# Storing the last slab of a rotary embedding whole instead of in two halves

## Chip, cores and metric

One core of one Trainium2 chip. The metric is the device time of one launch in microseconds (us), the median of several runs. The span in a profile is shorter by about 1.8 us (162.2 against 160.4 in the profiled run of the kernel before). Runs are marked fast or slow by state.

In the profile, a transfer's *issue* is the instruction that starts it, a *packet* is one piece of it (here one descriptor is one packet), and its *landing* is the moment when its completion is fully counted on its *semaphore*, a counter on which instructions can wait (in the traces each transfer makes 16 counts).

## The reference

`x` is (16, 512, 1024) float32, taken as 16 heads of 64; `cos` and `sin` are (512, 32).

```python
x1, x2 = x[..., :half_dim], x[..., half_dim:]
rotated = np.concatenate([
    x1 * cos - x2 * sin,
    x1 * sin + x2 * cos
], axis=-1)
```

33.55 MB come in and 33.55 MB go out, with a few operations for each element.

## The kernel before

The tensor is worked in 8 slabs of 4 MB: 128 partitions with 8192 float32 (32 KB) each. The kernel keeps five slabs on the chip (in SBUF). SyncE loads, ScalarE casts to bfloat16, VectorE does two multiplies and an add, ScalarE casts back and issues the store. The first slab and the last two are computed in halves of 4096 columns. The cuts are marked, here and in the diffs below; some comments are added.

```python
    def dram(t, s, a=0, n=W):          # a..a+n of each partition's 32 KB of slab s
        return bass.AP(tensor=t.tensor, offset=t.offset + s * nb * seq * dim + a,
                       ap=[[W, P], [1, n]])
    ...
    def load(s):
        slab[s] = slabs.tile([P, W], f32, tag="slab", name="slab")
        return nc.sync.dma_start(out=slab[s], in_=dram(x, s))
    ...
    passes = []
    for s in range(nslabs):
        n = rpp if 1 <= s < nslabs - 2 else rpp // 2
        passes += [(s, r, n) for r in range(0, rpp, n)]

    cast(passes[0])
    for i, (s, r, n) in enumerate(passes):
        if i + 1 < len(passes):
            cast(passes[i + 1])        # ScalarE, float32 to bfloat16
        ...                            # VectorE: two multiplies and an add
        back = nc.scalar.copy(out=xs, in_=xu)
        if s == nslabs - 1:
            if r > 0:
                ...                    # keep this copy behind the first half's issue
            part = nc.scalar.dma_start(
                out=dram(out_flat, s, r * dim, n * dim), in_=xs)
        elif r + n == rpp:
            nc.scalar.dma_start(out=dram(out_flat, s), in_=slab[s])
            if s + slots < nslabs:
                load(s + slots)
```

Of the kernel before, what the change touches and what calls it, by code (L numbers as in the profile page):

```python
# [2 lines left out]

# [4 lines left out]


@with_exitstack  # L10
def kernel(
    ctx: ExitStack,
    tc: tile.TileContext,
    x: bass.AP,
    cos: bass.AP,
    sin: bass.AP,
    num_heads: int,
    out: bass.AP,
):
    nc = tc.nc  # L20
    P = nc.NUM_PARTITIONS

    batch, seq, dim = x.shape
    nh = num_heads
    hd = dim // nh
    half = hd // 2
    bf16 = mybir.dt.bfloat16
    f32 = mybir.dt.float32

    nb = 2  # L30
    slots = 5
    nslabs = batch // nb
    rpp = nb * seq // P
    W = rpp * dim
    SP = seq // rpp
    TW = rpp * half

    out_flat = out.rearrange("b s h d -> b s (h d)")

    singles = ctx.enter_context(tc.tile_pool(name="singles", bufs=1))  # L40
    slabs = ctx.enter_context(tc.tile_pool(name="slabs", bufs=slots))
    xpool = ctx.enter_context(tc.tile_pool(name="xpool", bufs=2))
    psum = ctx.enter_context(tc.tile_pool(
        name="psum", bufs=1, space=bass.MemoryType.PSUM))


    def dram(t, s, a=0, n=W):
        return bass.AP(tensor=t.tensor, offset=t.offset + s * nb * seq * dim + a,
                       ap=[[W, P], [1, n]])


    def view(t, offset, *dims):
        return dataclasses.replace(t, offset=t.offset + offset,
                                   ap=[t.ap[0], *[list(d) for d in dims]])


    slab = {}
# [7 lines that stand above are left out]
    load(0)  # L65


    TR = seq // P
    G = rpp // TR
    table = {}  # L70
    raw = singles.tile([P, 2 * TR * half], f32, tag="raw")
    for i, src in enumerate((cos, sin)):
        table[i] = nc.gpsimd.dma_start(out=view(raw, i * TR * half, (1, TR * half)), in_=bass.AP(  # L73
            tensor=src.tensor, offset=src.offset,
            ap=[[TR * half, P], [1, TR * half]]))



    for s in range(1, slots):
        tc.add_manual_dep(  # L80
            load(s).ins, table[0].ins.name,
            mybir.DependencyInfo(mybir.DependencyClass.Sync,
                                 mybir.DependencyReason.DATA),
            reason="issue")



    pick = singles.tile([P, 2 * G * P], bf16, tag="pick")
    nc.gpsimd.memset(pick, 0.0)  # L89
    for g in range(2 * G):  # L90
        part = view(pick, g * P, (SP, P // SP), (1, SP))
        nc.gpsimd.affine_select(  # L92
            out=part, in_=part, compare_op=mybir.AluOpType.not_equal,
            fill=1.0 if g < G else -1.0, base=-(g % G),
            pattern=[[0, P // SP], [-G, SP]], channel_multiplier=1)

    tab1 = singles.tile([P, 2 * TR * half], bf16, tag="tab1")
    nc.gpsimd.tensor_copy(out=tab1, in_=raw)  # L98

    acc = psum.tile([P, 2 * rpp * hd], f32, tag="acc")  # L100
    for i in range(2):
        for h in range(2):
            for g in range(G):
                nc.tensor.matmul(  # L104
                    view(acc, (i * rpp + g * TR) * hd + h * half, (hd, TR), (1, half)),
                    view(pick, (i * h * G + g) * P, (1, P)),
                    view(tab1, i * TR * half, (half, TR), (1, half)),
                    start=True, stop=True)
    tab = singles.tile([P, 2 * rpp * hd], bf16, tag="tab")
    nc.vector.tensor_copy(out=tab, in_=acc)  # L110

    xb = {}


    def cast(u):
        s, r, n = u
        if r == 0:
            xb[s] = xpool.tile([P, W], bf16, tag="xb", name="xb")
        nc.scalar.copy(out=view(xb[s], r * dim, (1, n * dim)),  # L119
                       in_=view(slab[s], r * dim, (1, n * dim)))  # L120
# [13 lines that stand above are left out]
            cast(passes[i + 1])  # L134
        xs = view(slab[s], r * dim, (1, n * dim))
        xu = view(xb[s], r * dim, (1, n * dim))

        t2 = view(slab[s].bitcast(bf16), 2 * r * dim, (1, n * dim))
        for t, a in ((t2, rpp * hd), (xu, 0)):
            nc.vector.tensor_mul(  # L140
                out=t, in0=xu,
                in1=view(tab, a + r * hd, (hd, n), (0, nh), (1, hd)))
        nc.vector.tensor_add(  # L143
            out=xu, in0=xu, in1=view(t2, half, (hd, n * nh), (-half, 2), (1, half)))

        back = nc.scalar.copy(out=xs, in_=xu)  # L146
        if s == nslabs - 1:

            if r > 0:
                tc.add_manual_dep(  # L150
                    back.ins, part.ins.name,
                    mybir.DependencyInfo(mybir.DependencyClass.NoSync,
                                         mybir.DependencyReason.DATA),
                    reason="issue")
            part = nc.scalar.dma_start(
                out=dram(out_flat, s, r * dim, n * dim), in_=xs)
        elif r + n == rpp:
            nc.scalar.dma_start(out=dram(out_flat, s), in_=slab[s])
            if s + slots < nslabs:
                load(s + slots)  # L160


# [1 line left out]
_INS = ['x', 'cos', 'sin', 'num_heads']  # L164
_OUTS = [((16, 512, 16, 64), 'float32')]

_NUMBERS = {'num_heads': 16}


# [26 lines left out]
```

## Time and profile before

| | before |
|---|---|
| median of the 3 runs known at first | 162.57 us (162.40 to 162.63) |
| span of the profiled run | 160.4 us |
| VectorE, ScalarE busy | 68%, 71% |
| loads (q1), stores (q10), share of 16 DMA engines | 49.4%, 48.5% |

The two DMA queues together fill 98% of the span: this kernel moves bytes all the time, and neither compute engine is full. The lines themselves are in the prediction.

### The profile page before, as it was taken

The page shows a single profiled execution, that of the slowest core. Times are in us where ns is not written, and L with a number is a line of the kernel's source. Part 1 is how long each engine was busy: PE and PEld are TensorE (multiplying, and loading weights), DVE is VectorE, ACT ScalarE, POOL GpSimd, SP SyncE. Part 2 cuts the span into 40 slices and gives each one's busy share as a digit, 9 for nine tenths or more (in the row PEclk, how much of TensorE's full clock was granted, in tenths as well). Part 3 has the DMA queues.
Part 4 walks back from the last instruction along what each step waited for, and adds up shares of the span by engine and source line. Part 5 has one row for each costly group of instructions (what it writes and reads, how often), then busy time and mean ns, then how long its engine had stood idle before and what let it go on. Part 6 is the DMA issues. An engine that isn't in the chain of part 4 may idle for free.

```text
span 160.4 us, 169 instructions
## 1 busy us (share of the span) xinstructions
PE 1.0 (1%) x8; PEld 0.8 (1%) x8; DVE 108.5 (68%) x34; ACT 113.5 (71%) x23; POOL 3.4 (2%) x12
## 2 busy tenths in 40 slices
PE   0011000000000000000000000000000000000000
PEld 0010000000000000000000000000000000000000
DVE  0003799999989979997996099939649599920000
ACT  3006939998998999899907997099995999471000
POOL 7000000000000000000000000000000000000000
DMA  7999999999999999999999999999999999999994
GB/s 229 441 409 400 474 433 392 449 466 392 392 392 449 466 392 425 490 392 409 490 409 409 482 417 392 490 425 392 458 458 392 433 482 392 417 490 400 400 437 208
DMA packets 2512, 67.24 MB, mean 419 GB/s; under 512 B 304, under 2 KB 304, under 8 KB 336
## 3 DMA queue, kind: packets, MB, share of 16 engines
q1 hardware_dynamic: 1152, 33.55, 49.4%
q10 hardware_dynamic: 1296, 33.56, 48.5%
q0 software_dynamic: 64, 0.13, 0.2%
HBM read 33.69 MB, written 33.55 MB: 419 GB/s over the span
## 4 chain that ended last, share of the span: by engine, by line
DMA 59%; ACT 17%; issue 9%; DVE 4%; SPq 0%; POOLq 0%
DMA slab<-in_x_dram 40%; DMA out_dram<-slab 15%; ACT slab L146 11%; ACT xb L119 6%; DMA raw<-in_cos_dram 4%; DVE xb L143 1%; DVE xb L140 1%; DVE slab L140 1%; SPq L62 0%; POOLq L177 0%
## 5 line engine op out<-in xcount | busy, mean ns | idle before, releaser
L119 ACT CAST xb<-slab 128x4096 bf16<-128x4096 f32 (+1 forms) x11 | 56.6, 5155 | 27.4 <-DMA slab<-in_x_dram 26.1
L146 ACT CAST slab<-xb 128x4096 f32<-128x4096 bf16 (+1 forms) x11 | 56.6, 5153 | 3.4 <-DVE xb L143 3.4
L140 DVE TENSOR_TENSOR slab<-xb,tab 128x4096 bf16<-128x4096 bf16 (+1 forms) x11 | 35.9, 3260 | 19.7 <-ACT xb L119 19.6
L143 DVE TENSOR_TENSOR xb<-xb,slab 128x4096 bf16<-128x4096 bf16 (+1 forms) x11 | 35.9, 3261 | 0.3
L140 DVE TENSOR_TENSOR xb<-xb,tab 128x4096 bf16<-128x4096 bf16 (+1 forms) x11 | 35.9, 3260 | 0.3
L110 DVE CAST tab<-acc 128x1024 bf16<-128x1024 f32 x1 | 1.2, 1225 | 12.6 <-PE acc L104 12.6
L119 ACT ACT_TABLE_LOAD x1 | 1.3, 1283 | 0.7 <-PEq L177 0.7
L104 PE MATMUL acc<-tab,pick 128*128 128x128 bf16 x8 | 1.0, 305 | 11.6 <-POOL tab L98 11.6
L92 POOL TENSOR_SCALAR_AFFINE_SELECT pick<-pick 128x128 bf16<-128x128 bf16 x4 | 1.0, 289 | 0.1
L104 PEld LDWEIGHTS <-pick 128*128 128x128 bf16 x8 | 0.8, 136 | 11.4 <-issue 8.1
L73 POOL DMA_DIRECT2D raw<-in_cos_dram x1 | 0.7, 677 | 0.8 <-POOLq L177 0.8
L98 POOL CAST tab<-raw 128x256 bf16<-128x256 f32 x1 | 0.4, 398 | 7.0 <-DMA raw<-in_sin_dram 7.0
L89 POOL MEMSET pick<- 128x512 bf16 x1 | 0.5, 544 | 0.0
L73 POOL DMA_DIRECT2D raw<-in_sin_dram x1 | 0.5, 537 | 0.0
L177 POOL MEMSET const-float32-0.0<- 128x1 f32 x1 | 0.1, 99 | 0.2 <-issue 0.2
L177 POOL MEMSET const-bfloat16-1.0<- 128x1 bf16 x1 | 0.1, 102 | 0.0
L177 POOL MEMSET const-uint8-127<- 128x1 uint8 x1 | 0.1, 102 | 0.0
L177 POOL MEMSET const-float32-1.0<- 128x1 f32 x1 | 0.1, 99 | 0.0
## 6 DMA issues: line engine op xcount, KB each, us to landing
slab<-in_x_dram SPq DMA_DIRECT2D x8, 4096.0 KB, 24.6
out_dram<-slab ACTq DMA_DIRECT2D x7, 4096.0 KB, 27.8
out_dram<-slab ACTq DMA_DIRECT2D x2, 2048.0 KB, 15.3
raw<-in_cos_dram POOLq DMA_DIRECT2D x1, 64.0 KB, 7.1
raw<-in_sin_dram POOLq DMA_DIRECT2D x1, 64.0 KB, 9.1
```

The costliest lines, as they stand in the source:

```text
L73: table[i] = nc.gpsimd.dma_start(out=view(raw, i * TR * half, (1, TR * half)), in_=bass.AP(tensor=src.tensor, offset=src.offset, ap=[[TR * ...
L89: nc.gpsimd.memset(pick, 0.0)
L92: nc.gpsimd.affine_select(out=part, in_=part, compare_op=mybir.AluOpType.not_equal, fill=1.0 if g < G else -1.0, base=-(g % G), pattern=[[ ...
L98: nc.gpsimd.tensor_copy(out=tab1, in_=raw)
L104: nc.tensor.matmul(view(acc, (i * rpp + g * TR) * hd + h * half, (hd, TR), (1, half)), view(pick, (i * h * G + g) * P, (1, P)), view(tab1, ...
L110: nc.vector.tensor_copy(out=tab, in_=acc)
L119: nc.scalar.copy(out=view(xb[s], r * dim, (1, n * dim)), in_=view(slab[s], r * dim, (1, n * dim)))
L140: nc.vector.tensor_mul(out=t, in0=xu, in1=view(tab, a + r * hd, (hd, n), (0, nh), (1, hd)))
L143: nc.vector.tensor_add(out=xu, in0=xu, in1=view(t2, half, (hd, n * nh), (-half, 2), (1, half)))
L146: back = nc.scalar.copy(out=xs, in_=xu)
L177: nc = _bacc.Bacc("TRN2", target_bir_lowering=False, num_devices=1)
```

## The change

The intent is to move the last slab in the largest descriptors the layout allows, one of 32 KB for each partition, as for all other slabs, and to give up the early start of its first half in exchange.

```diff
-        back = nc.scalar.copy(out=xs, in_=xu)
-        if s == nslabs - 1:
-
-            if r > 0:
-                tc.add_manual_dep(
-                    back.ins, part.ins.name,
-                    mybir.DependencyInfo(mybir.DependencyClass.NoSync,
-                                         mybir.DependencyReason.DATA),
-                    reason="issue")
-            part = nc.scalar.dma_start(
-                out=dram(out_flat, s, r * dim, n * dim), in_=xs)
-        elif r + n == rpp:
+        nc.scalar.copy(out=xs, in_=xu)
+        if r + n == rpp:
             nc.scalar.dma_start(out=dram(out_flat, s), in_=slab[s])
```

## The prediction

> **What bounds the kernel now.** I read the page first, for who is busy, and in it the shares of the span, the slices and the DMA queues.
>
> ```profile
> span 160.4 us, 169 instructions
> ...
> DVE  0003799999989979997996099939649599920000
> ACT  3006939998998999899907997099995999471000
> ...
> DMA  7999999999999999999999999999999999999994
> ...
> DMA packets 2512, 67.24 MB, mean 419 GB/s; under 512 B 304, under 2 KB 304, under 8 KB 336
> ...
> q10 hardware_dynamic: 1296, 33.56, 48.5%
> ```
>
> The reader is to see that the DMA row holds 9 in every slice but the first and the last, while VectorE and ScalarE have fallen to 0 in the last three slices (about 12 us). The end is not set by the last computation but by transfers still under way. The queue q10 carries the stores; 1296 packets is 7 slabs x (128 descriptors + 16 end markers) = 1008, plus 2 halves x (128 + 16) = 288. So one descriptor is one packet, 32 KB in a whole slab and 16 KB in a half.
>
> Second, the timeline of the end, to see when the last stores are issued.
>
> ```profile
> 131.01 0.34 ACTq L158 DMA_DIRECT2D out_dram<-slab  x1
> ...
> 134.49 3.61 ACT L146 CAST slab<-xb 128x4096 f32<-128x4096 bf16 x1
> ...
> 138.12 0.34 ACTq L155 DMA_DIRECT2D out_dram<-slab  x1
> 139.17 2.29 DVE L143 TENSOR_TENSOR xb<-xb,slab 128x4096 bf16<-128x4096 bf16 x1
> 141.50 3.60 ACT L146 CAST slab<-xb 128x4096 f32<-128x4096 bf16 x1 [3.40 <-DVE xb L143]
> 145.13 0.34 ACTq L155 DMA_DIRECT2D out_dram<-slab  x1
> ```
>
> Slab 6 (the seventh of eight) is issued at 131.01, the first half of slab 7 at 138.12 and the second at 145.13. Third, the view of the output tensor for each of these three moments alone gives issue to landing; in this order:
>
> ```profile
> DMA to landing us min/median/max: 18.6/18.6/18.6
> ...
> DMA to landing us min/median/max: 16.4/16.4/16.4
> ...
> DMA to landing us min/median/max: 14.2/14.2/14.2
> ```
>
> So slab 6 lands at 131.01 + 18.6 = 149.6, the first half at 138.12 + 16.4 = 154.5 and the second at 145.13 + 14.2 = 159.3. The issues lie 7.0 us apart, but the landings 4.9 and 4.8 us: 2.1 MB in 4.85 us is 432 GB/s. The stores stand in line. When the second half is issued, slab 6 is still being written for 149.6 - 145.1 = 4.5 us, and the first half has not moved a byte. The chain of waits ends with the copy at 141.50 and ascribes nothing to that line of transfers, so it is not the view to trust here.
>
> Fourth, the stretches 130 to 148 and 149 to 158.4 (32 KB packets in the first, 16 KB in the second), with busy time of the engines, granted clock, DMA share and GB/s:
>
> ```profile
> 130.00:148.00 18.00, 0.00 (x0) 0.00 (x0) 11.29 (x5) 11.70 (x4) 0.00 (x0) 1.00 1.01 435
> 149.00:158.40 9.40, 0.00 (x0) 0.00 (x0) 0.00 (x0) 0.00 (x0) 0.00 (x0) 1.00 1.00 431
> ```
>
> All 16 engines are full in both. A share a hair over 1 is neighbouring packets that overlap a little and edges of the stretch.
>
> [...]
>
> **The change part by part.**
>
> Removed: the issue at 138.12, 0.34 us on ScalarE's sequencer. ScalarE has nothing to do then: its next copy waits 3.40 us for VectorE's add, which ends at 141.47. Worth 0. Removed too: the ordering of the second copy behind the first issue. The copy runs at 141.50 because of the add, so this is worth 0.
>
> Moved: the first half's bytes are offered at 145.13 instead of 138.12, 7.0 us later. This is the suspected cost. It is paid only if the engines run out of work before. When do they? In the DMA view of the stretch 148.6 to 149.4, in 40 slices of 0.02 us (packets count at their start), all 16 end markers of slab 6 appear, and the first packet of the half is in slice 8:
>
> ```profile
> GB/s 0 0 0 0 0 0 0 1638 0 0 0 819 0 819 819 0 819 819 0 1639 1639 0 819 0 0 819 819 0 0 0 819 0 819 0 0 0 0 1638 0 0
> DMA packets 34, 0.29 MB, mean 369 GB/s; under 512 B 16, under 2 KB 16, under 8 KB 16
> ```
>
> That is 148.6 + 7 x 0.02 = 148.74 for the first engine and about 149.26 for the last (one slot in each engine, before its second packet). From issue to first packet on an idle core: the first load is issued at 0.74 (timeline), and the DMA view of 0 to 2.5 shows its first packet in slice 29 of 0.0625 us, at 1.75. That is 1.0 us. The whole slab issued at 145.13 should have its first descriptors ready at 146.1, which is 2.6 us before the first engine wants one. Cost: 0.
>
> Changed: 256 packets of 16 KB become 128 of 32 KB, and one set of 16 end markers goes. From the DMA view of 120 to 137 (q10: 236 packets, 16 of them markers, 98.2% of 16 engines) a 32 KB packet takes 0.982 x 16 x 17 / 220 = 1.214 us. From the view of 149.5 to 158 (239 packets, 16 markers, 100.3%) a 16 KB packet takes 1.003 x 16 x 8.5 / 223 = 0.612 us. Two of these are 1.223, 9 ns more than one large one. Each engine has 8 such pairs one after another on the path: 8 x 9 = 72 ns, and a marker less, which moves 4 bytes and counts little. An upper value, since the packets overlap a little: a gain of 0.08 us, and I take 0.05.
>
> Sum: 0 + 0 + 0 - 0.05 us. 162.57 - 0.05 = 162.52, told as 162.5. That is 0.03% and a quarter of the spread of the runs before (162.40 to 162.63).
>
> **The rivals.** First, **the late start shows in full**: who takes the last computation for the end would say that half a slab, 4.85 us, now waits until 145.13 and comes on top: 167.4 us, 3% slower. Against it: the two halves are issued with 4.5 us of slab 6 still ahead. And even on an empty queue a slab issued at 145.13 would end at 145.13 + 1.0 + 9.7 + 0.4 (last packet to landing, an estimate: the last 16 KB packets start near 158.35 and last 0.61, and the landing is at 159.3) = 156.2, sooner than the bytes ahead of it allow. What sets the end is the number of bytes.
>
> Second, **a bubble between the two stores**: the new issue could be held back until slab 6 has landed[...]. Then the first packet would come at 149.6 + 1.0 = 150.6 instead of 148.74, and the time would be 162.5 + 1.9 = 164.4 us, which is 1.2% and still inside 2%. Against it: in the kernel before, two or three stores stand in line on this queue without a gap.
>
> Third, **large descriptors pay more than I say**[...]. To reach 2% they would have to save 3.25 of the 9.7 us of the last slab; the 32 KB stretch moves 435 GB/s against 431, which is 1% of 9.7 us, 0.1 us. So 162.4 at best.
>
> Fourth, the scheduler may order ScalarE's last instructions otherwise, now that the forced order is gone. The last copy has to wait for the last add anyway; there are 2.6 us of slack to hide a small shift.
>
> **Range and chances.** The sum gives 162.5. Runs of before spread over 0.23 us[...]. So 162.1 to 162.9 should hold it 8 times in 10. The bubble, at 164.4, gets about 5%, and leaves the verdict at within 2%. Slower by over 2% needs the issue to come after the queue has drained and some 3 us more: 1%. Faster by over 2% has no source: 1%. Within 2%: 98%.
>
> **What would show it right or wrong.** In the changed kernel's profile: one issue of 4096 KB at about 145.1 and none at 138.1; q10 with 1296 - 144 = 1152 packets and the same bytes; the copy still at 141.5 behind VectorE; the DMA row at 9 without a dip near 148.7; landing at about 159.3, 14.1 us after the issue, so the median of issue to landing for this last store as for the second half before; a span of 160.3 to 160.4. A dip of the DMA share between 148.7 and 151 would show the bubble, and a 32 KB packet at other than 1.21 us in the last 10 us would show the size step wrong. The prediction fails if the last store's first packet comes later than 148.7, or if something before 138 us moves, which no part of the change asks for.

The sum came to 162.57 - 0.05 = 162.52 us. That the engines are full at the end rests on the table of the two stretches alone (share 1.01 and 1.00, 435 and 431 GB/s). The width of the range is the author's guess; the runs known then spread over 0.23 us.

## The result

| | before | after |
|---|---|---|
| median of 6 runs each | 162.43 us (162.31 to 162.63) | 162.09 us (161.95 to 162.30) |
| ratio of fast runs | | 0.9979, 95% interval 0.9967 to 0.9992 |
| span of the profiled run | 160.4 us | 160.4 us |

A ratio is the mean time of one kernel's fast runs over the mean of the other's in the same rounds, so it is not quite the ratio of the medians. Executions over 1.5% slower than the fastest of the same kernel are left out of the means. The change is within 2%, as forecast, but the gain is real: 0.34 us by the medians, where 0.05 had been predicted, and 162.09 lies a hair below the stated range of 162.1 to 162.9.

The page of the changed kernel, lines for span, DMA row, packets and store queue:

```profile
span 160.4 us, 169 instructions
...
DMA  7999999999999999999999999999999999999995
...
DMA packets 2368, 67.24 MB, mean 419 GB/s; under 512 B 288, under 2 KB 288, under 8 KB 320
...
q10 hardware_dynamic: 1152, 33.55, 48.4%
```

144 packets fewer (2512 to 2368; on q10 1296 to 1152: 128 of data and 16 end markers, which the traces' records have at 4 bytes and 9 ns each), the same bytes, no dip in the DMA row. Its timeline at the end:

```profile
131.10 0.34 ACTq L148 DMA_DIRECT2D out_dram<-slab  x1
...
139.26 2.29 DVE L143 TENSOR_TENSOR xb<-xb,slab 128x4096 bf16<-128x4096 bf16 x1
141.64 3.60 ACT L146 CAST slab<-xb 128x4096 f32<-128x4096 bf16 x1 [3.46 <-DVE xb L143]
145.28 0.34 ACTq L148 DMA_DIRECT2D out_dram<-slab  x1
```

The issue near 138 is gone, and the last copy still waits for VectorE. From issue to landing, for the store at 131.10 and then for the one at 145.28 (view of the output tensor):

```profile
DMA to landing us min/median/max: 18.7/18.7/18.7
...
DMA to landing us min/median/max: 14.2/14.2/14.2
```

Slab 6 lands at 149.8 and slab 7 at 159.5; there is no bubble. The two stretches that the prediction compared:

```profile
130.00:148.00 18.00, 0.00 (x0) 0.00 (x0) 11.38 (x5) 11.79 (x4) 0.00 (x0) 1.00 0.99 426
149.00:158.40 9.40, 0.00 (x0) 0.00 (x0) 0.00 (x0) 0.00 (x0) 0.00 (x0) 1.00 1.01 436
```

So far nearly every sign that the prediction named came true, the span included, and yet the time fell by more than it should. The exception is small: the last slab's first packet starts at 148.84, where the prediction had allowed 148.7, but it follows slab 6's last packet on its engine without a gap (that one ends at 148.85; slab 6 was later in this run), so it is no bubble. The span of a single profile is of no help at this size: within one kernel the spans of its runs differ by 0.6 us or more (before: 160.5 to 161.1 over 42 runs, median 160.6; after: 160.1 to 160.8 over 18, median 160.35).

What differs lies behind the last landing, a place the prediction did not look at. The times with three decimals here are read from the records in the traces, which the views round. The last landing is recorded at 159.321 before and 159.498 after, the end of the span at 160.427 and 160.381. From the last landing to the end it is **1.106 us before and 0.883 after**: 0.223 us less. In the two profiled runs this was hidden, because slab 6 happened to land 0.225 us later in the changed kernel's run (149.840 against 149.615). The waits of SyncE from 123 us on, summed, with their number and the longest, before:

```profile
SPq L191 <- DMA out_dram<-slab: 35.4, 1, 35.4
```

and after:

```profile
SPq L181 <- DMA out_dram<-slab: 35.3, 4, 9.6
```

Before, SyncE stands in one single wait for 35.4 us; after, in four waits of at most 9.6 us. These are the waits that close the program (their line is that of the closing of the program's context). The view of that line between 159.3 and 159.76, before:

```profile
L191 SPq EVENT_SEMAPHORE  x5: 28/28/35408, 123.9 to 159.6; - x5
L191 SPq DRAIN  x2: 7/7/7, 159.6 to 159.7; - x2
```

and after:

```profile
L181 SPq DRAIN  x2: 7/7/7, 159.6 to 159.6; - x2
...
L181 SPq EVENT_SEMAPHORE  x1: 27/27/27, 159.5 to 159.5; - x1
```

Before, the long wait is followed by four more waits that are already satisfied; their starts in the trace are 159.377, 159.441, 159.503 and 159.562, and the drain comes at 159.630, so each takes some 62 ns. After, one is left. From the drain to the end of the span it is 0.797 us before and 0.799 after, so the whole difference lies in these waits. The semaphores say why; the traces' records number them for every transfer and every wait. The transfers on q1 and q10, which the page calls hardware_dynamic (hardware-issued below), count on eight semaphores, 107, 111 and 113 to 118, here called H0 to H7. In the changed kernel each of the eight gets 32 counts, those of two transfers; in the kernel before H0 gets 48. Both programs end with six waits of SyncE in the order of these numbers (two semaphores in some waits, others left out):

```
            17 hardware-issued DMAs (before)       16 (after)
            last half of slab 7 counts on H0       slab 7 counts on H7
end wait 1  H2, H1                                 H2, H1
end wait 2  H3, H0  <- ends last                   H3, H0
end wait 3  H4                                     H4
end wait 4  H5                                     H5
end wait 5  H6                                     H6
end wait 6  H7                                     H7      <- ends last
```

Eight loads and nine stores make 17. In the order of the compiled program they take the eight in turn, so the last store wraps round to H0, and the other four waits are stepped through after it (159.377 to 159.630). With one store less the last one is on H7.

### The profile page after: what moved, and what is told of

The parts are those of the page before. It is cut to its first block, busy times and chain, and to the rows that moved or that the text cites. A ratio compares the mean times of both kernels' runs of the same rounds, so it can differ in the third digit from the quotient of the medians.

```text
span 160.4 us, 169 instructions
## 1 busy us (share of the span) xinstructions
PE 1.0 (1%) x8; PEld 0.8 (1%) x8; DVE 108.5 (68%) x34; ACT 113.5 (71%) x23; POOL 3.4 (2%) x12
## 2 busy tenths in 40 slices
DMA packets 2368, 67.24 MB, mean 419 GB/s; under 512 B 288, under 2 KB 288, under 8 KB 320
## 3 DMA queue, kind: packets, MB, share of 16 engines
q1 hardware_dynamic: 1152, 33.55, 49.5%
q10 hardware_dynamic: 1152, 33.55, 48.4%
## 4 chain that ended last, share of the span: by engine, by line
DMA 59%; ACT 17%; issue 9%; DVE 4%; SPq 0%; ACTq 0%; POOLq 0%
DMA slab<-in_x_dram 39%; DMA out_dram<-slab 15%; ACT slab L146 11%; ACT xb L119 6%; DMA raw<-in_cos_dram 4%; DVE xb L140 1%; DVE xb L143 1%; DVE slab L140 1%; SPq L62 0%; ACTq L146 0%; POOLq L167 0%
## 5 line engine op out<-in xcount | busy, mean ns | idle before, releaser
L104 PE MATMUL acc<-tab,pick 128*128 128x128 bf16 x8 | 1.0, 305 | 11.5 <-POOL tab L98 11.5
```

What stands on the lines that cost most here:

```text
L104: nc.tensor.matmul(view(acc, (i * rpp + g * TR) * hd + h * half, (hd, TR), (1, half)), view(pick, (i * h * G + g) * P, (1, P)), view(tab1, ...
```

## The experiments

**Theory E**: the gain comes from the order of the end waits (0.22 us) and the packets give 0.05 us. **Rival P**: the 32 KB packets give all of it. **Rival N**: it is drift between runs. The prediction's slack (2.6 us between the late issue and the moment the engines need it) is tested too. A semaphore is chosen here by changing the number of hardware-issued DMAs. All kernels gave correct results.

### First try: eight tiny loads (w8, w9, h7, h8)

```diff
+    spare = singles.tile([16, 16], f32, tag="spare")
+    for k in range(8):                    # w8: 8, w9: 9, h7: 7, h8: 8
+        nc.sync.dma_start(
+            out=view(spare, k, (1, 1)), in_=bass.AP(
+                tensor=cos.tensor, offset=cos.offset + k,
+                ap=[[TR * half, 16], [1, 1]]))
```

w8 and w9 have it in the changed kernel, h7 and h8 in the kernel before.

> Whole slab in the last store, plus 8 tiny loads (16 elements of 4 bytes each, never used) issued from SyncE behind the first five loads. The hardware-issued DMAs take 8 completion semaphores in turn; with 24 of them the last store is on the last semaphore that SyncE waits for at the end, as in the changed kernel (16 of them). Theory E (the end waits): one wait after the last landing, last landing to end of span 0.88 us, time as the changed kernel plus at most 0.1 us for the tiny loads: 162.1 to 162.2, ratio to before 0.998. Rival P (the 32 KB packets themselves save the 0.3 us): the same time, so this run alone does not tell them apart; w9 does. Rival N (the 0.34 us is drift between runs): equal to before.

> As w8 with one tiny load more (9): now 25 hardware-issued DMAs, so the last store wraps round to the first semaphore, and SyncE meets it in the second of its six end waits, as in the kernel before. Theory E: four waits of 62 ns come after the last landing, last landing to end 1.10 us instead of 0.88, time 0.2 to 0.25 us above w8 although the last store is whole in 32 KB packets. Rival P: within 0.05 us of w8. Rival N: all equal.

> The kernel before (two halves of 16 KB) plus 7 tiny loads: 24 hardware-issued DMAs, so the last half is on the last semaphore. Theory E: one wait after the last landing, last landing to end 0.88 us; faster than before by 0.2 us less the tiny loads' cost, and within 0.1 us of w8 (0.05 us for the packets). Rival P: as slow as before, 0.3 us above w8.

> The kernel before plus 8 tiny loads: 25 hardware-issued DMAs, the last half on the first semaphore again. The control for h7: Theory E: 0.2 to 0.25 us above h7, last landing to end 1.10 us. Rival P: equal to h7. The tiny loads themselves show as h8 less before: 0 to 0.1 us.

The times were a miss for every theory: 166.74, 166.94, 167.33 and 167.12 us (ratios of fast runs 1.028 to 1.030; w8's runs at 167.99 and 168.01 are slow, its four fast ones took 165.20 to 166.78). The tiny loads hold SyncE until 63 us, as most of them wait for the earlier user of their semaphore (in w8 five waits for loads of whole slabs, 34.3 us together, and one of 15.8 us for a store), and in w8 the sixth slab's load is issued at 63.09 instead of 61.35.

ScalarE loses more. Its second store counts, by w8's compiled program, on the semaphore of the second tiny load (H7). That load was issued at 10.53 but landed only at 63.00, after the last of the five slab loads issued ahead of it (62.65), and the store waited for it. In w8's timeline:

```profile
63.08 0.36 ACTq L155 DMA_DIRECT2D out_dram<-slab  x1
...
63.48 7.02 ACT L126 CAST xb<-slab 128x8192 bf16<-128x8192 f32 x1 [12.06 <-DMA spare<-in_cos_dram]
```

In the kernel before, the second store goes out 11.5 us earlier:

```profile
51.59 0.34 ACTq L158 DMA_DIRECT2D out_dram<-slab  x1
```

From 61 to 65 us the DMA engines then move only 148 GB/s in w8 (148, 156 and 123 in w9, h7 and h8), against 393 in the kernel before. At the 430 GB/s that w8 reaches from 100 to 130 us, the bytes missing there are worth 2.6 us, an estimate; w8's profiled span is 3.0 us longer than that of the kernel before. Where the rest of the loss comes from was not followed up. The times tell nothing about 0.2 us, but the ends of the profiles do. SyncE's waits in w8 (24 hardware-issued DMAs, whole slab):

```profile
SPq L188 <- DMA out_dram<-slab: 34.8, 4, 9.6
```

in w9 (25, whole slab):

```profile
SPq L188 <- DMA out_dram<-slab: 55.6, 1, 55.6
```

in h7 (24, halves):

```profile
SPq L198 <- DMA out_dram<-slab: 34.9, 5, 9.7
```

and in h8 (25, halves):

```profile
SPq L198 <- DMA out_dram<-slab: 33.8, 1, 33.8
```

Whole or halved, the store's place among the semaphores alone sets the pattern. The last landing is 0.881 us from the end in w8 and h7, and 1.107 us in w9 and h8.

### The same with little disturbance (w1, hsw)

w1 is the changed kernel with one tiny load behind the last slab's load, where nothing waits for it before the end (the line that makes the tile `spare` is cut):

```diff
             if s + slots < nslabs:
                 load(s + slots)
+                if s + slots == nslabs - 1:
+                    nc.sync.dma_start(out=spare, in_=bass.AP(
+                        tensor=cos.tensor, offset=cos.offset,
+                        ap=[[TR * half, 16], [1, 1]]))
```

> The changed kernel plus one tiny load (16 elements of 4 bytes, never used), issued from SyncE right behind the last slab's load, where nothing waits for it before the end: the eight tiny loads of w8 held up the sixth slab's load and cost 4 us, which swamped the times. With 17 hardware-issued DMAs the last store is on the first completion semaphore again. Theory E: last landing to end 1.10 us instead of 0.88, time 0.2 to 0.25 us above the changed kernel, so equal to the kernel before within 0.1 us (ratio 0.9985 to 1.0003), though the last store is whole. Rival P (32 KB packets save the 0.3 us): as the changed kernel, ratio 0.998.

hsw is the kernel before with its first half on GpSimd's queue, which counts on other semaphores (its two table loads on 99 and 100 in the traces of both kernels):

```diff
-            part = nc.scalar.dma_start(
+            part = (nc.gpsimd if r == 0 else nc.scalar).dma_start(
```

> The kernel before, in two halves of 16 KB, with the first half issued from GpSimd instead of ScalarE: its completion is then counted on a semaphore of the other kind and 16 hardware-issued DMAs are left, so the second half is on the last semaphore. Theory E: last landing to end 0.88 us, time 0.2 us below before, 0.05 us above the changed kernel: ratio 0.9982 to 0.999. [...] Rival P: as before, ratio 1.000.

In hsw slab 6 landed 23.7 us after its issue, against 18.6 in the kernel before.

w1: 162.43 us, ratio to before 0.9997 (0.9984 to 1.0009). hsw: 162.21 us, ratio 0.9986 (0.9974 to 0.9999). Both as Theory E has it. The closing line in w1, from 159.3 to 159.76:

```profile
L186 SPq EVENT_SEMAPHORE  x5: 28/28/33880, 125.5 to 159.6; - x5
```

and in hsw:

```profile
L191 SPq EVENT_SEMAPHORE  x1: 28/28/28, 159.5 to 159.5; - x1
```

The whole slab with the store on H0 has the five waits of the kernel before; the halves with the store on H7 have the one of the changed kernel.

### The changed kernel again, the packet size, and the slack (a_again, p4k, q4k, d2, d4, d8)

> The changed kernel once more, unchanged, for the size of the effect: Theory E plus the packets: 0.2 to 0.3 us below before, ratio 0.998 to 0.9987. Rival N (drift): within 0.1 us of before.

a_again: 162.19 us, ratio 0.9984 (0.9972 to 0.9996). This speaks against drift, but its interval overlaps those of w1 and hsw.

p4k was meant to cut the last store into 4 KB descriptors with an access pattern of eight adjoining pieces, `ap=[[W, P], [c, W // c], [1, c]]` with `c = 1024`.

> The changed kernel with the last store, still one DMA, cut into 4 KB descriptors (8 for each partition). Only the size of packets changes, not the order of the end waits. If a packet costs 4 to 5 ns on top of its bytes, as the difference between two 16 KB and one 32 KB packet says, each engine has 56 packets more: 0.25 us slower than the changed kernel. Rival P, with 0.3 us for 8 packets more for each engine (37 ns a packet): 2.1 us slower. If the two adjoining runs are merged into one descriptor again, the packet count stays at 1152 and nothing is learnt.

Its page shows 2368 packets: the pieces were merged again. It is therefore only one more run of the changed kernel, at 162.16 us and ratio 0.9979. q4k takes the pieces from the last to the first:

```diff
+            if s == nslabs - 1:
+                c = W // 8                # q16k below: W // 2, two pieces
+                nc.scalar.dma_start(
+                    out=bass.AP(tensor=out_flat.tensor,
+                                offset=out_flat.offset + s * nb * seq * dim + W - c,
+                                ap=[[W, P], [-c, 8], [1, c]]),
+                    in_=view(slab[s], W - c, (-c, 8), (1, c)))
+            else:
                 nc.scalar.dma_start(out=dram(out_flat, s), in_=slab[s])
```

> The changed kernel with the last store, still one DMA and on the same semaphore, cut into eight 4 KB pieces for each partition, taken from the last to the first so that they are not merged again (as they were in p4k, whose packet count stayed at 2368). 16 x 56 = 896 packets more. At 4.5 ns a packet on top of its bytes (two 16 KB packets 1214 ns apart from start to start, one of 32 KB 1209.5): 0.25 us slower than the changed kernel, last landing to end 0.88. Rival P (0.3 us for 8 packets more on each engine): 2 us slower.

q4k: 162.54 us, ratio 0.9999 (0.9987 to 1.0012). Its page:

```profile
DMA packets 3264, 67.24 MB, mean 419 GB/s; under 512 B 288, under 2 KB 288, under 8 KB 1344
```

There are 3264 - 2368 = 896 packets more. From slab 6's last landing to slab 7's it is 9.944 us, against 9.659 in a_again: 0.285 us for 56 packets more on each engine, **5.1 ns a packet**. Rival P's 37 ns (0.3 us for 8 packets more on each engine) is out by far.

d2, d4 and d8 delay the last issue with needless copies:

```diff
         nc.scalar.copy(out=xs, in_=xu)
+        if s == nslabs - 1 and r > 0:
+            for m in (2,):                # d4: (4,)   d8: (4, 4)
+                nc.scalar.copy(out=view(slab[s], r * dim, (1, m * dim)),
+                               in_=view(xb[s], r * dim, (1, m * dim)))
```

> The changed kernel with one needless copy of 1.8 us (half of the last half again) on ScalarE before the last store, which is then issued at about 147.1 instead of 145.2. The prediction gave the late issue 2.6 us of slack: no change, within 0.1 us of the changed kernel. If the issue needs more than 1.7 us to reach the engines, or if the rival of a bubble is right in part: a DMA gap near 148.8 and up to 1.9 us more.

> The same with a needless copy of 3.6 us: issue at about 148.9. With 1.0 us from issue to first packet the engines, done with slab 6 from 148.8 to 149.4, wait until 149.9: a gap of about 1.0 us, time 0.8 to 1.1 us above the changed kernel. If the slack is larger than thought: less.

> The changed kernel with two needless copies of 3.6 us on ScalarE before the last store: issue at 151.8 to 152.4. d4 (issue at 148.19) left gaps of 0.07 to 0.15 us on five of the engines, whose first packet of the last slab then came at about 149.05, 0.86 us after the issue. So here the first packets come 0.9 us after the issue, at about 152.7, against 148.9 to 149.4 without a gap: 3.3 to 3.6 us slower than the changed kernel, and the DMA row shows the gap.

d2, issued at 146.49: 162.20 us, no change. d4: 162.24 us, no change either, where 0.8 to 1.1 us had been expected. That estimate took the issue to be at 148.9; ScalarE was earlier in this run (a_again issues at 144.54, not 145.28), and it came at 148.19. The DMA view of d4 from 148.6 to 149.4, GB/s in slices of 0.02 us:

```profile
GB/s 0 0 0 0 0 0 0 0 0 0 0 0 0 0 0 0 0 0 0 0 0 0 8192 1638 0 0 0 0 3277 0 3277 0 0 0 1639 1639 1638 0 0 0
```

Five packets start together in slice 23, at 148.6 + 22 x 0.02 = 149.04. These are engines that had been done with slab 6 since about 148.92 and had stood idle for 0.07 to 0.15 us: the late issue is just at the edge. From issue to first packet it took 149.04 - 148.19 = 0.85 us. d8 goes past the edge: 165.58 us, ratio 1.0191, 3.4 us above a_again (another chip), as expected. Its issue in the timeline:

```profile
151.90 0.34 ACTq L152 DMA_DIRECT2D out_dram<-slab  x1
```

and its DMA view from 152.4 to 153.2:

```profile
GB/s 0 0 0 0 0 0 0 0 0 0 0 0 0 0 0 0 1638 6554 3277 1638 3277 4915 1638 1638 1638 0 0 0 0 0 0 0 0 0 0 0 0 0 0 0
```

The first packet starts in slice 17, at 152.72, 0.82 us after the issue. So in the changed kernel the first packet of the last slab could have come at 145.28 + 0.85 = 146.1, and no engine wanted one before 148.84 (in its DMA view of 148.6 to 149.4): 2.7 us of slack, against 2.6 predicted.

### All in the same rounds (a_side, w1_side, hsw_side, q16k)

The intervals of a_again, w1 and hsw overlap, and a_again stems from other rounds than the two. So the three ran again side by side, unedited, with q16k: the changed kernel with 16 KB packets and everything else left alone.

> The changed kernel, as the reference for the other three on the same chip and in the same rounds: 0.2 to 0.3 us below before. Last landing to end 0.88 us; last landing of slab 6 to last landing of slab 7 9.66 us, as in the two traces of it so far (9.658 and 9.659).

> Whole slab, last store on the first semaphore, by one tiny load more. Theory E: 0.2 to 0.3 us above a_side, last landing to end 1.10. If the end waits are not the cause: equal to a_side.

> Two halves, last half on the last semaphore. Theory E: 0.2 us below before, at most 0.1 us above a_side; last landing to end 0.88 to 0.89. If the packets are the cause: equal to before.

> The changed kernel with the last store as one DMA of two 16 KB pieces for each partition, second piece first, so that only the packet size of the change is undone, with the end waits left as in the changed kernel. At 4.5 to 5.1 ns a packet: slab 6's last landing to slab 7's 9.70 us instead of 9.66, last landing to end 0.88, time 0.04 us above a_side, which the times cannot resolve. Rival P: 0.3 us above a_side, as before.

| kernel | packets of the last slab | last store on | median us | ratio to before | last landing to end, us | slab 6's last landing to slab 7's, us |
|---|---|---|---|---|---|---|
| before (time: same rounds) | 16 KB, two stores | H0 | 162.36 | 1 | 1.106 | 9.706 |
| a_side | 32 KB | H7 | 162.04 | 0.9976 (0.9963 to 0.9989) | 0.882 | 9.680 |
| w1_side | 32 KB | H0 | 162.56 | 1.0004 (0.9991 to 1.0017) | 1.107 | 9.666 |
| hsw_side | 16 KB, two stores | H7 | 162.21 | 0.9984 (0.9972 to 0.9996) | 0.892 | (mixed) |
| q16k | 16 KB, one store | H7 | 162.19 | 0.9990 (0.9977 to 1.0004) | 0.882 | 9.714 |

a_side and w1_side now have intervals apart (0.9989 and 0.9991 at the nearest), a hair's breadth: the same 32 KB store is slow with its semaphore on H0 and fast on H7.

But the two lie 0.52 us apart by their medians, more than twice what the end waits explain. In the two profiled runs (spans of 160.745 and 160.360) 0.225 us of the 0.385 lie behind the last landing; 0.174 lie before slab 6's landing (149.972 against 149.798). Slab 6's landing also varies between the traces of other kernels (149.681 in w1, 149.717 in p4k, 149.839 in a_again), so this part is not put down to the semaphore; whether the tiny load adds to it is not shown.

hsw_side keeps the halves and still gains. q16k's interval includes 1, so its time alone decides nothing, but its median is on the fast side and its end is the short one. The packets are what is left: 9.714 against 9.680 here and 9.659 in a_again, 0.03 to 0.06 us. All traces together say it better: this time is 9.658 to 9.680 us in the ten with the slab in 32 KB packets (d8, whose store comes too late, left out), and 9.698 to 9.723 in the four with 16 KB on the same queue (before, h7, h8, q16k); the means, 9.668 and 9.710, are 0.042 us apart. The page of q16k confirms that the 16 KB packets were made:

```profile
DMA packets 2496, 67.24 MB, mean 419 GB/s; under 512 B 288, under 2 KB 288, under 8 KB 320
```

No version beat the changed kernel: its last store is already on the semaphore waited for last.

## Why the prediction was wrong

It was right on the path that it followed, up to the last landing, and it left out a term behind it.

- **What bounds the end** (a line of stores at full rate): right for the last landing. The DMA row holds 9 up to the last slice, and the stretch from 149.0 to 158.4 runs at 436 GB/s. It is not the whole truth that "What sets the end is the number of bytes": 1.106 us of closing follow the last landing, and the change made them 0.883.
- **Removed issue and ordering, worth 0**: right for ScalarE. But the removed issue was also one hardware-issued DMA of 17, and in that role it was worth 0.22 us. **This is the step that failed**: "Removed: the issue at 138.12 ... Worth 0." The sum "0 + 0 + 0 - 0.05 us" ought to have had -0.22 in its first place: with one DMA fewer the last store is on H7, which SyncE waits for last, and from last landing to end it is 0.883 us instead of 1.106.
- **Moved, 2.6 us of slack, cost 0**: right. d2 and d4 used it up without loss that the times show, d8 went beyond it and paid 3.4 us. The 1.0 us from issue to first packet measured 0.82 to 0.85.
- **Changed packets, 0.05 us taken**: right. 9.706 us before and 9.658 after, 0.048 us (0.042 over all traces). The working was less good than its result: a packet's fixed cost is 5.1 ns by q4k, where the prediction, with one packet more in a pair, had 9 ns out of two rounded shares. Its 0.05 instead of the 0.08 worked out was a guess, and partly luck.
- **Rivals**: no bubble, no late start, and 32 KB packets pay no more than told. None of the four named the end of the program.
- **The range**: the centre was 0.41 us above the measured 162.09. Of this, 0.22 us are the end waits; 0.14 us are the base, whose median was 162.57 in the three runs known then and 162.43 in six. The rest, about 0.05 us, is within the noise of one median. That 162.09 fell just outside the range is chance: further runs of the same kernel had medians of 162.19 (a_again) and 162.16 (p4k), inside it, and 162.04 (a_side), outside. The missing term is not chance; it is in every trace. That the span came out at 160.4, as foretold, is luck: slab 6 landed later by as much as the end waits saved.

Of the gain (0.34, 0.25 and 0.32 us by medians in three sets of rounds), the traces account for 0.22 + 0.05 = 0.27 us. Whether the remainder is only noise cannot be told at this spread. That the end waits cause the larger part is shown in two ways: by the traces, where the time from last landing to end follows the semaphore in all 18 profiles (0.881 to 0.892 us in the 13 with the last store on H7, 1.106 or 1.107 in the five with it on H0), and by a_side against w1_side in time, in direction rather than in size.

## What to carry to other kernels

Where transfers stand in line until the end, as here, the moment of the last issue was free until the line ran out (2.7 us of slack; d8 went past it and paid 3.4 us); read the slack from landings and first packets, not from the compute timeline. Where a change alters the number of DMAs, look also at which completion semaphore the last one lands on and at what the program does after the last landing: here a wait on an already finished store cost some 62 ns when it came after the long wait, and nothing when it came before. A gain of 0.2% is not to be read from two single profiles; split the span at events that both traces have, here the last landing, and compare the parts.

Two more numbers from the runs. From the start of the issuing instruction to the first packet of a 128-partition transfer it was 0.82 us (d8, engines idle), 0.85 us (d4) and 1.0 us (the first load of the kernel before); of this the instruction itself took 0.34 to 0.37 us. And a tiny transfer held up another engine's through a shared completion semaphore: in w8 ScalarE's second store waited for a load of 64 bytes and went out at 63.08 us instead of 51.59.
